# Block inverse: one product over a zero-kept triangle, and products that alternate between row groups and banks

## The chip, the cores and the metric

The kernel runs on one core of a Trainium2 chip. The metric is the time of one execution on the device in microseconds (us). TensorE (PE) multiplies matrices and writes its results to PSUM, VectorE (DVE) and ScalarE (ACT) bring them from there to SBUF, GpSimd (POOL) does small work in SBUF, and SyncE (SP) issues the transfers. Each engine works through its own instructions in order and waits on semaphores of the others.

## The reference

The reference is a stack of blocks over 1024 positions and 1024 channels. The change lies in one of them, a gated delta rule with 8 heads of width 128, cut to what matters here:

```
a_mat = where(strict, (k_beta @ k^T) * decay_mask, 0)     # per head and chunk
t_mat = triangular_solve(a_mat + eye, eye, lower=True)     # its inverse
w = t_mat @ (k_beta * exp(g));  u = t_mat @ v_beta
# then, chunk after chunk:
v_new = u - w @ state
o = q_dec @ state + attn @ v_new
state = state * e_last + k_dec^T @ v_new
```

The kernel uses chunks of 128 positions, so a head has 8 chunks, and 8 lower triangles of 128x128 have to be inverted for each head.

## The kernel before

Most of the kernel's time goes to projections in which a float32 operand is split into two float16 parts (`mm_chT`, lines 111 to 113, and `mm_t`, lines 118 to 120): three products for one. The delta rule lies in the stretch from about 400 to 1000 us. There the program is written head by head: `stage1` (transposes, k·k and q·k products), `base` (blocks of 32x32 inverted by forward substitution on DVE), `levels` (joins the blocks), `chain` (the eight chunks in turn), and `dense(h+2)`, the projections for the head after the next one. In the last heads `zgate`, another projection, takes the place of `dense`. A scheduler of the language sets the order of each engine's instructions from that program; so the projections of `dense` and `zgate` come to stand on TensorE between the small products of `levels` and `chain`.

`levels` holds the inverse of each 128x128 triangle in two layouts: `TdT`, the inverse transposed (an upper triangle), and `Td`, its 32x32 blocks transposed in place. The four diagonal blocks come from `base` through DRAM. Three steps follow. In the first, pairs of blocks of 32 are joined to halves of 64: `ps_x` (line 783) multiplies the block of the strict triangle `U` by one inverse, `X` (784) takes it out of PSUM, `ps_t1` (787) and `ps_t1t` (790) multiply it by the other inverse, for each of the two layouts, and lines 788 and 791 write the results with a minus sign into `Td` and `TdT`. In the second, the two halves are joined: `ps_x2` (796, 797), its copy `X2` (798), `ps_t2t` (801) and its result in `TdT` (802). In the third, `ps_u` and `ps_w` (810) use the finished inverse. The PSUM tiles come from `ps_c`, three banks that are used in turn. In the order and in the trace all the names that begin with ps_t1 or X lose their digit where buffer numbers are left out: `ps_x` is also ps_x2, `ps_t` is ps_t1, `X` is also X2.

Every float32 product shows in the trace as two records of a matmul, so 8 products are 16 records. Operands of 32 rows and 32 columns use one of the sixteen 32x32 parts of the array, those of 64 one of the four 64x64 parts; the part is set by the partitions of the operands (rows) and of the result (columns).

Of the kernel before, what the change touches and what calls it, by code (L numbers as in the profile page):

```python
# [12 lines left out]
AF = mybir.ActivationFunctionType  # L13
ALU = mybir.AluOpType
# [7 lines left out]
NT = 8  # L22
# [6 lines left out]
def kernel(ctx, tc, ins, out):  # L29
    nc = tc.nc  # L30
    pe, dve, act, pool, sp = nc.tensor, nc.vector, nc.scalar, nc.gpsimd, nc.sync
    a = ins
# [16 lines left out]
    def ps_c(n="psc"):  # L49
        return psmm.tile([P, 512], F32, tag="c", name=n, bufs=3)  # L50
# [234 lines left out]
    # ======================= layer 0 =======================  # L285
# [280 lines left out]
    # ======================= layer 1 =======================  # L566
# [14 lines left out]
    with ExitStack() as s0:  # L581
        pl = mkpool("gdn", stack=s0)
        gcol = mkpool("gdnc", stack=s0)
        # decay and beta columns
        wab = load_w(in_w, 4 * D, ncols=16)
        psab = ps_c("ps_ab")
        for i in range(NT):
# [7 lines left out]
        beta = gcol.tile([P, NT, NH], F32, name="beta")  # L595
# [6 lines left out]
                                 op0=ALU.mult, op1=ALU.mult)  # L602
        # exp(-104) is 0 in float32, and so is every decay over such a step
# [22 lines left out]
        TdTs = [pl.tile([P, NT, P], F32, name=f"TdT{i}") for i in range(2)]  # L626
# [5 lines left out]
        # identity columns of the base solves  # L632
# [118 lines left out]
        def base(h):  # L751
            # blocks of 32 by forward substitution, one column group of 8 per partition group
            Lp = st_[h]["Lp"]
            tpd = tp_d[h % 2]
            Tt = gcol.tile([P, 8, 32], F32, tag="Tt", name="Tt")
            tm = gcol.tile([P, 8, 32], F32, tag="tm", name="tm")
            pool.tensor_copy(Tt, tinit)
            for j in range(31):
                n = 31 - j
                tv = tm[:, :, :n]  # L760
                dve.tensor_tensor(out=tv, in0=Lp[:, j, j + 1:].unsqueeze(1).to_broadcast([P, 8, n]),  # L761
                                  in1=Tt[:, :, j:j + 1].to_broadcast([P, 8, n]), op=ALU.mult)
                dve.tensor_tensor(out=Tt[:, :, j + 1:], in0=Tt[:, :, j + 1:], in1=tv, op=ALU.subtract)  # L763
            for q in range(4):
                sp.dma_start(tpd.rearrange("b c m i -> (b c) m i")[:, 8 * q:8 * q + 8, :], Tt[32 * q:32 * q + 32])
            for b in range(4):
                sp.dma_start(TdTs[h % 2][32 * b:32 * b + 32, :, 32 * b:32 * b + 32], tpd[b].rearrange("c m i -> m c i"))

        def levels(h):
            d = st_[h]  # L770
            U, kr, vr, Dc = d["U"], d["kr"], d["vr"], d["Dc"]
            TdT = TdTs[h % 2]
# [3 lines left out]
            # pairs of blocks of 32  # L776
            X = pl.tile([P, NT, 32], F32, tag="X", name="X")
            px, p1, p1t = ps_c("ps_x"), ps_c("ps_t1"), ps_c("ps_t1t")
            v32 = [p[:, :256].rearrange("p (c t) -> p c t", c=NT) for p in (px, p1, p1t)]
            blk = [(slice(r, r + 32), slice(r + 32, r + 64)) for r in (0, 64)]  # L780
            for A, B in blk:
                for c in range(NT):
                    pe.matmul(v32[0][B, c, :], U[A, c, B], Td[A, c, A], start=True, stop=True)
                act.activation(X[B], v32[0][B], AF.Copy)
            for A, B in blk:
                for c in range(NT):
                    pe.matmul(v32[1][B, c, :], TdT[B, c, B], X[B, c, :], start=True, stop=True)
                dve.tensor_scalar(out=Td[B, :, A], in0=v32[1][B], scalar1=-1.0, scalar2=None, op0=ALU.mult)
                for c in range(NT):
                    pe.matmul(v32[2][A, c, :], X[B, c, :], TdT[B, c, B], start=True, stop=True)  # L790
                act.activation(TdT[A, :, B], v32[2][A], AF.Copy, scale=-1.0)
            # halves of 64
            X2 = pl.tile([P, NT, 64], F32, tag="X2", name="X2")
            px = ps_c("ps_x2").rearrange("p (c t) -> p c t", c=NT)
            for c in range(NT):
                pe.matmul(px[hi, c, 0:32], U[lo, c, hi], Td[lo, c, 0:32], start=True, stop=True)
                pe.matmul(px[hi, c, 32:64], U[32:64, c, hi], Td[32:64, c, 32:64], start=True, stop=True)
# [152 lines left out]
    # ======================= hybrid block =======================  # L950
    w_in = a["w_in_2"][0]
    G32, PS, HS, NB = 32, 64, 16, 4
    with ExitStack() as s2:
# [39 lines left out]
        with ExitStack() as s5:  # L993
# [8 lines left out]
            with ExitStack() as s6:  # L1002
# [32 lines left out]
                # growth: exp(lr dt) - 1 through tanh, and its powers  # L1035
# [9 lines left out]
                # angle in turns, range reduced, in two exact parts  # L1045
# [13 lines left out]
                # powers 7..0 and 0..8  # L1059
# [38 lines left out]
                # input matrix: (abar - 1) / lambda * b  # L1098
# [33 lines left out]
                # signed power tables per half  # L1132
# [9 lines left out]
                # skip term on the diagonal of the first tap  # L1142
# [34 lines left out]
            def s5_batch(b):  # L1177
# [6 lines left out]
                # parameters of this batch of groups  # L1184
# [20 lines left out]
                # transposed input maps  # L1205
# [8 lines left out]
                # causal kernel inside a chunk  # L1214
# [14 lines left out]
                # rotation tables and decays  # L1229
# [11 lines left out]
                # inputs by chunk  # L1241
# [278 lines left out]
```

## Time and profile before

| | |
|---|---|
| runs (us) | 1912.77, 1914.98, 1927.49; median 1914.98 |
| profiled execution: span from the first to the last instruction (us), which is the time known of it | 1914.6 |
| TensorE busy, its share of the span | 1808.0 us, 94% |
| DVE, ACT, POOL busy | 76%, 49%, 3% |
| granted TensorE clock, mean over the span | 0.960 |

A busy TensorE is one with a matmul under way; the ends of matmuls are modelled, and the start of the next record tells more of how fast they follow each other than the duration of one. The granted clock is the share of the full 2.4 GHz: 1.00 is that, 0.50 is 1.2 GHz.

### The profile page before, as it was taken

The page shows a single profiled execution, that of the slowest core. Times are in us where ns is not written, and L with a number is a line of the kernel's source. Part 1 is how long each engine was busy: PE and PEld are TensorE (multiplying, and loading weights), DVE is VectorE, ACT ScalarE, POOL GpSimd, SP SyncE. Part 2 cuts the span into 40 slices and gives each one's busy share as a digit, 9 for nine tenths or more (in the row PEclk, how much of TensorE's full clock was granted, in tenths as well). Part 3 has the DMA queues.
Part 4 walks back from the last instruction along what each step waited for, and adds up shares of the span by engine and source line. Part 5 has one row for each costly group of instructions (what it writes and reads, how often), then busy time and mean ns, then how long its engine had stood idle before and what let it go on. Part 6 is the DMA issues. An engine that isn't in the chain of part 4 may idle for free.

```text
span 1914.6 us, 29618 instructions
## 1 busy us (share of the span) xinstructions
PE 1808.0 (94%) x11847; PEld 1133.6 (59%) x11847; DVE 1450.2 (76%) x2472; ACT 935.7 (49%) x1673; POOL 52.8 (3%) x130
## 2 busy tenths in 40 slices
PE   5799789999899999999999999899999999999998
PEld 3344338855466656687878859556444444444487
DVE  6898876655786678877637689999999999594333
ACT  6567563356555666666434443465463121482221
POOL 0000001000000000001000020000000000000000
PEclk8899899999988899999889999999999999999999
DMA  9343255313131131224324322111221112102212
GB/s 336 108 154 85 93 154 188 105 52 84 31 88 39 27 102 30 79 78 138 91 93 155 115 37 71 38 51 53 92 75 54 57 56 77 45 23 66 78 67 89
DMA packets 161635, 165.26 MB, mean 86 GB/s; under 512 B 45662, under 2 KB 139934, under 8 KB 161498
## 3 DMA queue, kind: packets, MB, share of 16 engines
q1 hardware_dynamic: 161498, 163.38, 27.5%
q8 instruction: 93, 1.52, 0.3%
q14 instruction: 44, 0.36, 0.1%
HBM read 139.05 MB, written 23.12 MB: 85 GB/s over the span
## 4 chain that ended last, share of the span: by engine, by line
PE 51%; DVE 29%; ACT 7%; DMA 6%; issue 6%; SPq 1%; POOL 0%; DVEq 0%; ACTq 0%; POOLq 0%
DVE cc L990 5%; PE psmm L112 3%; PE psmm L111 3%; PE psmm L113 3%; DVE wl L105 2%; DMA wst_ada<-in_ada_w_dram 2%; PE ps_out L120 2%; PE ps_out L118 2%; PE ps_out L119 2%; DVE Tt L763 2%; DVE tm L761 2%; PE ps_fin L118 1%; PE ps_fin L120 1%; PE ps_fin L119 1%; PE ps_zc L113 1%
## 5 line engine op out<-in xcount | busy, mean ns | idle before, releaser
L111 PE MATMUL psmm<-hTh,wh 128*128 128x512 f16 x896 | 347.3, 389 | 19.9 <-ACT zs L515 16.7
L112 PE MATMUL psmm<-hTl,wh 128*128 128x512 f16 x896 | 347.6, 388 | 0.1
L113 PE MATMUL psmm<-hTh,wl 128*128 128x512 f16 x896 | 346.4, 387 | 0.0
L990 DVE SCALAR_TENSOR_TENSOR cc<-cu,cols,cc 128x1024 f32<-128x1024 f32 (+1 forms) x270 | 302.2, 1170 | 0.9
L112 PEld LDWEIGHTS <-wh 128*128 128x128 f16 x1568 | 155.0, 99 | 194.7 <-issue 29.5
L113 PEld LDWEIGHTS <-wl 128*128 128x128 f16 x1568 | 155.1, 99 | 179.3 <-issue 13.4
L111 PEld LDWEIGHTS <-wh 128*128 128x128 f16 x1568 | 155.1, 99 | 178.0 <-issue 12.0
L105 DVE SCALAR_TENSOR_TENSOR wl<-wst,wh 128x2048 f16<-128x2048 f32 (+2 forms) x71 | 154.3, 2177 | 57.8 <-ACT wh L104 57.6
L104 ACT ACTIVATE wh<-wst 128x2048 f16<-128x2048 f32 (+2 forms) x71 | 128.6, 1813 | 116.8 <-PE ps_gs L112 27.7
L763 DVE TENSOR_TENSOR Tt<-Tt,tm 128x248 f32<-128x248 f32 (+30 forms) x248 | 77.7, 313 | 4.5
L761 DVE TENSOR_TENSOR tm<-Lp,Tt 128x248 f32<-128x248 f32 (+30 forms) x248 | 76.9, 310 | 4.2
L118 PE MATMUL ps_z<-wh,hTh 128*128 128x256 f16 x256 | 72.1, 282 | 0.0
L119 PE MATMUL ps_z<-wh,hTl 128*128 128x256 f16 x256 | 72.0, 281 | 0.0
L120 PE MATMUL ps_z<-wl,hTh 128*128 128x256 f16 x256 | 71.9, 281 | 0.0
L120 PE MATMUL ps_out<-wl,y 128*128 128x256 f16 x256 | 69.8, 273 | 0.1
L118 PE MATMUL ps_fin<-wh,merged 128*128 128x256 f16 x256 | 69.8, 273 | 0.0
L119 PE MATMUL ps_fin<-wh,merged 128*128 128x256 f16 x256 | 69.8, 273 | 0.0
L120 PE MATMUL ps_fin<-wl,merged 128*128 128x256 f16 x256 | 69.8, 273 | 0.0
L118 PE MATMUL ps_out<-wh,y 128*128 128x256 f16 x256 | 69.7, 273 | 0.0
L119 PE MATMUL ps_out<-wh,y 128*128 128x256 f16 x256 | 69.7, 273 | 0.0
L123 ACT ACTIVATE hTh<-ps_ht 128x512 f16<-128x512 f32 x32 | 17.3, 594 | 83.2 <-PE ps_ht L252 83.2
L701 ACT ACTIVATE jk<-ps_tk 128x128 f32<-128x128 f32 x128 | 35.7, 279 | 39.7 <-PE ps_tk L697 36.7
(535 smaller groups left out, 4171.7 us busy)
## 6 DMA issues: line engine op xcount, KB each, us to landing
wst<-in_w_in_dram SPq DMA_DIRECT2D x24, 1024.0 KB
wst_ada<-in_ada_w_dram SPq DMA_DIRECT2D x16, 1024.0 KB
wst<-in_gdn_in_w_dram SPq DMA_DIRECT2D x16, 1024.0 KB
xt<-in_x_dram SPq DMA_DIRECT2D x16, 512.0 KB
wst<-in_lru_in_w_dram SPq DMA_DIRECT2D x8, 1024.0 KB
sta<-in_ada_w_dram SPq DMA_DIRECT2D x8, 1024.0 KB
x_d<-xt SPq DMA_DIRECT2D x16, 512.0 KB
wst<-in_lru_out_w_dram SPq DMA_DIRECT2D x4, 1024.0 KB
```

Source lines behind the costliest of these rows:

```text
L104: act.activation(hi, st, AF.Copy, scale=WS)
L105: dve.scalar_tensor_tensor(out=lo, in0=st, scalar=WS, in1=hi, op0=ALU.mult, op1=ALU.subtract)
L111: pe.matmul(ps, wh[:, k, c0:c0 + P], ah(k), start=(k == 0), stop=False)
L112: pe.matmul(ps, wh[:, k, c0:c0 + P], al(k), start=False, stop=False)
L113: pe.matmul(ps, wl[:, k, c0:c0 + P], ah(k), start=False, stop=(k == nk - 1))
L118: pe.matmul(ps, ah(k), wh[:, k, :], start=(k == 0), stop=False)
L119: pe.matmul(ps, al(k), wh[:, k, :], start=False, stop=False)
L120: pe.matmul(ps, ah(k), wl[:, k, :], start=False, stop=(k == nk - 1))
L701: act.activation(jk, pst[:, P * c:P * (c + 1)], AF.Square, accum_out=kq[:, n, 4 * b + c:4 * b + c + 1])
L761: dve.tensor_tensor(out=tv, in0=Lp[:, j, j + 1:].unsqueeze(1).to_broadcast([P, 8, n]), in1=Tt[:, :, j:j + 1].to_broadcast([P, 8, n]), op=A ...
L763: dve.tensor_tensor(out=Tt[:, :, j + 1:], in0=Tt[:, :, j + 1:], in1=tv, op=ALU.subtract)
L990: dve.scalar_tensor_tensor(out=acc, in0=cus[j][:, i + t0:i + t0 + n], scalar=col("cw", j, i), in1=acc, op0=ALU.mult, op1=ALU.add)
```

## The change

In `levels` the pairs of blocks of 32 no longer come one after the other. The products of line 783 go to two PSUM tiles instead of one, chunk by chunk in turn between the two pairs; the second pair's copy goes to DVE instead of ACT. The products into `ps_t1` and `ps_t1t` stand in turn too, `ps_t1` of one pair beside `ps_t1t` of the other, so that neighbours use other rows of the array and another bank. The evictions come after all of them.

The join of the halves had two products for each chunk, because the block right above the diagonal of `TdT`'s first half is not zero after the first step of the head two before it (`TdT` is used by every second head). Now POOL sets that block to zero again for every head from the third on, and one product over all 64 rows takes the place of the two. All other differences are comments that are left out.

```diff
             pool.tensor_copy(Tt, tinit)
+            if h >= 2:
+                pool.memset(TdTs[h % 2][0:32, :, 32:64], 0.0)
...
-            px, p1, p1t = ps_c("ps_x"), ps_c("ps_t1"), ps_c("ps_t1t")
-            v32 = [p[:, :256].rearrange("p (c t) -> p c t", c=NT) for p in (px, p1, p1t)]
+            def v32(p):
+                return p[:, :256].rearrange("p (c t) -> p c t", c=NT)
             blk = [(slice(r, r + 32), slice(r + 32, r + 64)) for r in (0, 64)]
-            for A, B in blk:
-                for c in range(NT):
-                    pe.matmul(v32[0][B, c, :], U[A, c, B], Td[A, c, A], start=True, stop=True)
-                act.activation(X[B], v32[0][B], AF.Copy)
-            for A, B in blk:
-                for c in range(NT):
-                    pe.matmul(v32[1][B, c, :], TdT[B, c, B], X[B, c, :], start=True, stop=True)
-                dve.tensor_scalar(out=Td[B, :, A], in0=v32[1][B], scalar1=-1.0, scalar2=None, op0=ALU.mult)
-                for c in range(NT):
-                    pe.matmul(v32[2][A, c, :], X[B, c, :], TdT[B, c, B], start=True, stop=True)
-                act.activation(TdT[A, :, B], v32[2][A], AF.Copy, scale=-1.0)
+            pxs = [v32(ps_c("ps_x")) for _ in blk]
+            for c in range(NT):
+                for (A, B), px in zip(blk, pxs):
+                    pe.matmul(px[B, c, :], U[A, c, B], Td[A, c, A], start=True, stop=True)
+            for n, ((A, B), px) in enumerate(zip(blk, pxs)):
+                if n == 0:
+                    act.activation(X[B], px[B], AF.Copy)
+                else:
+                    dve.tensor_copy(X[B], px[B])
+            p1, p1t = v32(ps_c("ps_t1")), v32(ps_c("ps_t1t"))
+            def t1(n, c):
+                A, B = blk[n]
+                pe.matmul(p1[B, c, :], TdT[B, c, B], X[B, c, :], start=True, stop=True)
+            def t1t(n, c):
+                A, B = blk[n]
+                pe.matmul(p1t[A, c, :], X[B, c, :], TdT[B, c, B], start=True, stop=True)
+            for n in range(2):
+                for c in range(NT):
+                    t1(n, c)
+                    t1t(1 - n, c)
+            for A, B in blk:
+                dve.tensor_scalar(out=Td[B, :, A], in0=p1[B], scalar1=-1.0, scalar2=None, op0=ALU.mult)
+                act.activation(TdT[A, :, B], p1t[A], AF.Copy, scale=-1.0)
...
             for c in range(NT):
-                pe.matmul(px[hi, c, 0:32], U[lo, c, hi], Td[lo, c, 0:32], start=True, stop=True)
-                pe.matmul(px[hi, c, 32:64], U[32:64, c, hi], Td[32:64, c, 32:64], start=True, stop=True)
+                pe.matmul(px[hi, c, :], U[lo, c, hi], Td[lo, c, 0:64], start=True, stop=True)
             dve.tensor_copy(X2[hi], px[hi])
```

The numbers of the changed kernel's lines are higher by 3 in `base`, and by 19 behind the change: 783 is 789 there, 787 and 790 are 799 and 803, 796 and 797 are 816, 801 is 820 and 810 is 829; the evictions 784 are 792 and 794, 788 is 810, 798 is 817, 802 is 821.

Two places show what moves. The first is TensorE in the second head, from the second pair's ps_x to ps_t2t. Before (`psmm` is a projection of `dense`, `ps_qk` a q·k product of `stage1`):

```order
L783 MATMUL ps_x<-Td,U 32x32 x8
L787 MATMUL ps_t_4836<-X,TdT_3594 32x32 x8
L790 MATMUL ps_t1t<-TdT_3594,X 32x32 x8
L113 LDWEIGHTS wl
L113 MATMUL psmm<-hTh,wl 128x512
L745 MATMUL ps_qk<-qT,kT 128x128
L787 MATMUL ps_t_4836<-X,TdT_3594 32x32 x8
L790 MATMUL ps_t1t<-TdT_3594,X 32x32 x8
L796 MATMUL ps_x_4893<-Td,U 64x32
L797 MATMUL ps_x_4893<-Td,U 64x32
```

The same engine and head in the changed kernel, from the last of the 32 alternating products of lines 799 and 803 on:

```order
L799 MATMUL ps_t_4848<-X,TdT_3594 32x32
L803 MATMUL ps_t1t<-TdT_3594,X 32x32
L745 MATMUL ps_qk<-qT,kT 128x128 x3
L816 MATMUL ps_x_4887<-Td,U 64x64 x8
L745 MATMUL ps_qk<-qT,kT 128x128
L111 LDWEIGHTS wh
L111 MATMUL psmm<-hTh,wh 128x512
L112 LDWEIGHTS wh
L112 MATMUL psmm<-hTl,wh 128x512
L745 MATMUL ps_qk<-qT,kT 128x128 x4
```

Three q·k products now stand between the small products and the join, and the rest of them, which stood behind 16 products of lines 796 and 797, is shared out before and behind 8 products of line 816.

The second place is DVE in the same head, from the transposition of `TdT` on. Before (`vT` on line 667 is the convolution of a projection, which no product of this head's levels waits for):

```order
L733 TENSOR_SCALAR rq<-rq 128x8
L667 SCALAR_TENSOR_TENSOR vT<-xp,cols,vT 128x1024
L788 TENSOR_SCALAR Td<-ps_t_4836 32x8x32
L667 SCALAR_TENSOR_TENSOR vT<-xp,cols,vT 128x1024
L788 TENSOR_SCALAR Td<-ps_t_4836 32x8x32
L798 COPY X_4892<-ps_x_4893 64x512
```

And in the changed kernel:

```order
L733 TENSOR_SCALAR rq<-rq 128x8
L794 COPY X<-ps_x 32x256
L667 SCALAR_TENSOR_TENSOR vT<-xp,cols,vT 128x1024
L810 TENSOR_SCALAR Td<-ps_t_4848 32x8x32 x2
L667 SCALAR_TENSOR_TENSOR vT<-xp,cols,vT 128x1024
L817 COPY X_4886<-ps_x_4887 64x512
```

DVE gets one more eviction, and both evictions of `ps_t1` stand together, with a convolution before and one behind them.

## Rows read from the trace of the kernel before

**Rows 1.** The page: busy time and share by engine; share of the chain that ended last.

```profile
PE 1808.0 (94%) x11847; PEld 1133.6 (59%) x11847; DVE 1450.2 (76%) x2472; ACT 935.7 (49%) x1673; POOL 52.8 (3%) x130
...
PE 51%; DVE 29%; ACT 7%; DMA 6%; issue 6%; SPq 1%; POOL 0%; DVEq 0%; ACTq 0%; POOLq 0%
```

**Rows 2.** Stretch with all heads: us, busy of each engine, granted clock, DMA.

```profile
400.00:1000.00 600.00, 581.45 (x4233) 399.64 (x4232) 416.77 (x1075) 349.53 (x906) 25.72 (x47) 0.93 0.25 71
```

**Rows 3.** The eight level blocks, first ps_x to last ps_w: fourth head, and sum.

```profile
709.67:728.69 19.02, 19.02 (x210) 15.04 (x210) 12.31 (x16) 10.31 (x22) 0.20 (x2) 0.91 0.11 29
...
sum 167.32, PE 167.31 PEld 135.85 DVE 88.39 ACT 76.25 POOL 0.61; mean PE 20.91 PEld 16.98 DVE 11.05 ACT 9.53 POOL 0.08
```

**Rows 4.** Waits from 400 to 1000 us: total us, times, longest.

```profile
PE ps_tk L697 <- DVE U L715: 10.8, 5, 5.5
...
DVE X L798 <- PE ps_x L797: 39.3, 8, 6.1
...
DVE TdT L802 <- PE ps_t2t L801: 15.0, 8, 3.0
```

**Rows 5.** Stretches of lines 796 and 797, all eight heads: sum.

```profile
sum 39.36, PE 39.36 PEld 32.12 DVE 1.92 ACT 9.13 POOL 0.00; mean PE 4.37 PEld 3.57 DVE 0.21 ACT 1.01 POOL 0.00
```

**Rows 6.** TensorE in the fourth head by time: start us, duration us, what.

```profile
709.67 0.69 PE L783 MATMUL ps_x<-Td,U 32*32 32x32 f32 x16
710.29 0.39 PE L113 MATMUL psmm<-hTh,wl 128*128 128x512 f16 x1
...
711.28 0.59 PE L783 MATMUL ps_x<-Td,U 32*32 32x32 f32 x13
711.68 0.21 PE L787 MATMUL ps_t<-X,TdT 32*32 32x32 f32 x1
...
711.77 0.19 PE L783 MATMUL ps_x<-Td,U 32*32 32x32 f32 x1
711.80 0.48 PE L787 MATMUL ps_t<-X,TdT 32*32 32x32 f32 x10
...
714.49 0.30 PE L796 MATMUL ps_x<-Td,U 64*64 64x32 f32 x2
714.72 0.30 PE L797 MATMUL ps_x<-Td,U 32*64 32x32 f32 x2
...
721.66 1.14 PE L801 MATMUL ps_t2t<-TdT,X 64*64 64x64 f32 x16
722.74 0.39 PE L111 MATMUL psmm<-hTh,wh 128*128 128x512 f16 x1
```

**Rows 7.** The same engine in the first head, at the granted clock 0.50.

```profile
528.97 0.63 PE L113 MATMUL psmm<-hTh,wl 128*128 128x512 f16 x1
...
529.39 0.63 PE L111 MATMUL psmm<-hTh,wh 128*128 128x512 f16 x1
...
531.24 1.97 PE L801 MATMUL ps_t2t<-TdT,X 64*64 64x64 f32 x16
```

**Rows 8.** The 25 stretches of lines 783, 787 and 790, all eight heads: sum.

```profile
sum 25.63, PE 25.62 PEld 24.54 DVE 13.70 ACT 12.46 POOL 0.20; mean PE 1.02 PEld 0.98 DVE 0.55 ACT 0.50 POOL 0.01
```

**Rows 9.** Behind lines 796, 797 at half clock: first of eight stretches, last, sum.

```profile
528.14:536.97 8.83, 8.83 (x34) 4.03 (x34) 6.46 (x10) 0.00 (x0) 0.00 (x0) 0.50 0.57 147
...
970.27:977.29 7.02, 7.02 (x41) 5.69 (x41) 2.68 (x5) 0.60 (x1) 0.00 (x0) 0.50 0.00 0
sum 49.05, PE 49.05 PEld 35.99 DVE 33.39 ACT 10.75 POOL 0.30; mean PE 6.13 PEld 4.50 DVE 4.17 ACT 1.34 POOL 0.04
```

**Rows 10.** DVE operations: duration ns min/median/max, first and last start us.

```profile
L788 DVE TENSOR_SCALAR Td<-ps_t x16: 417/424/430, 521.9 to 963.8; 32x256 f32<-32x256 f32 x16
...
L798 DVE COPY X<-ps_x x8: 694/695/695, 528.2 to 970.4; 64x512 f32<-64x512 f32 x8
...
L802 DVE TENSOR_SCALAR TdT<-ps_t2t x8: 682/683/683, 533.2 to 974.1; 64x512 f32<-64x512 f32 x8
...
L667 DVE SCALAR_TENSOR_TENSOR vT<-xp,cols,vT x24: 1245/1285/1286, 425.0 to 841.9; 128x1024 f32<-128x1024 f32 x24
```

## The prediction

> **What bounds the kernel now.** I read the page first: TensorE is busy for 94% of the span and holds 51% of the chain that ended last, DVE 76% and 29% [rows 1]. Shares over the whole span hide stages, so next came the stretch that holds all eight heads: of 600 us TensorE is busy 581, DVE 417, ACT 350, POOL 26 [rows 2]. Then the level blocks alone, from the first ps_x of a head to its last ps_w: in the sum of eight, 167.32 us, TensorE is busy for 167.31 and DVE for 88 [rows 3]. The waits say the same from the other side: TensorE's longest wait in the stretch sums to 10.8 us, and not in these blocks, while DVE stands still 39.3 us for the products of lines 796 and 797 and 15.0 us for line 801 [rows 4]. So in these blocks TensorE sets the time, and what it no longer does there comes off the end, as long as the evictions keep up. The projections beside them are work that has to be done anyway; they hide nothing, they queue on the same engine.
>
> Two things make the blocks slow. The products are small, and TensorE's clock falls in or just before lines 796 and 797 of every head: eight stretches behind them, 49.05 us in all, run at 0.50, which is 1.2 GHz [rows 9]. A projection product follows the last one after 0.42 us there [rows 7], where at the full clock it is about half of that.
>
> **The change, part by part.** *The join of the halves.* Lines 796 and 797 now take 39.36 us in the eight heads [rows 5]. At the full clock one of these products costs 0.23 us (714.49 to 714.72), at 64*64 and 32*64 in turn. Line 801 shows what 8 products cost that stay in one shape: 721.66 to 722.74, 1.08 us, 0.135 us each, though each moves 64 columns and not 32 [rows 6]. The new line 816 is 8 products of just that shape. I take 1.08 us a head: 8 x 1.08 = 8.6, a gain of 39.4 - 8.6 = 30.7 us. If they run at half clock, 1.97 us a head [rows 7], the gain is 23.6; if it was not the change of shape that cost, 8 x 8 x 0.23 = 14.7, and the gain is 24.7.
>
> *The products of 32.* They take 25.63 us in all [rows 8], 3.2 us a head for 48 products, 96 records. Inside one line records follow each other by 0.40/13 = 0.031 us, and a stretch costs some 0.12 more when it begins (709.67 to 710.29 is 0.62 for 16). Where the stream passes from the second pair's ps_x to the first pair's ps_t1, other rows and another bank, six records start between 711.68 and 711.80: 0.02 us each, the two lines running beside each other at 0.03 each [rows 6]. If the alternating streams keep 0.016 to 0.02, a head costs 96 x 0.018 + 0.24 = 2.0 us, 16 in all, gain 9.7; if they don't, 96 x 0.031 + 0.24 = 3.2 and the gain is 0. The six are few and had been waiting in the queue, so I take a gain of 8. The Trainium skill (TensorE: Matmul & The Clock Gate, section "Wait — 56ns, not 53.3ns?") says that starts of matmuls never come closer than about 25 ns, however short they are; the starts in the trace, 0.02 apart, are closer than that. By the page alone 96 records cost 2.4 and 0.24 us, and the gain would be some 4 us instead of 8.
>
> *The clock.* With three quarters of lines 796 and 797 gone and projections or q·k products put between, TensorE has less small work in one piece. At worst the clock falls in every head as now, at best in none: then half of the 49.05 us comes back, 24.5. In the fourth head, where twelve q·k products stand between the products of 32, the clock stays up until the last product of line 797, and its blocks take 19.02 us at a mean of 0.91 where the mean of the eight is 20.9 [rows 3]. The changed order mixes like that in heads two to six, so I take two thirds, 16 us.
>
> *New waits.* There are four handovers in a head: X, the two Td, X2, TdT. An eviction takes 0.42, 0.7 or 0.68 us on DVE, and a convolution of 1.28 may stand before it [rows 10]. What covers them on TensorE is less than before: three projections (0.63 us at half of 0.42) behind ps_x, three q·k products behind the alternating ones, where both Td take 0.85 us. The second X copy is new on DVE, 0.42 us a head at most (the price of line 788, an eviction of the same size). The X2 copy has two projections and five q·k products behind line 816 as cover, for its 0.69 us, so nothing there; without them it would be 0.69 a head, 5.6. Beyond the cover I count 0.35 us for X, 0.35 for Td and 0.3 for TdT: 1 us a head, 8 us in all. From below it is 0, since DVE has 167.3 - 88.4 = 79 us free in these blocks [rows 3]; from above 2 us a head, 16, if a convolution stands in the way at each second handover. Behind the waiting evictions DVE has only convolutions and the next head's substitution queued, which it does later instead.
>
> *What costs nothing.* POOL sets the block to zero six times; it is busy 26 of 600 us [rows 2], the block is free once the head two before is through, and only this head's transposition of TdT waits for it; at worst each of the six holds a head up by 25.72/47 = 0.5 us, 3 in all. The two PSUM tiles for ps_x instead of one take a fourth turn of three banks; the first of them has been copied out before ps_t1t needs it, because ps_t1t reads that copy's neighbour. SP's loads of two weights move by a few places; TensorE's longest wait here is on DVE and not on a transfer [rows 4]. The zero triangle adds no columns: 64 moved for one product instead of 32 twice.
>
> The sum: -30.7 - 8 - 16 + 8 = -46.7 us, of the profiled execution's 1914.6: 1867.9. The median of the runs is 1914.98, 0.4 more, so the forecast is **1868 us**, 2.4% faster. By the bounds it lies between 1914.6 - 30.7 - 9.7 - 24.5 = 1850 and 1914.6 - 23.6 + 16 = 1907.
>
> **Rivals.** *The clock falls as before* (1.). The small products still stand closer together than projections do, and new waits put idle time between them. For it: behind the join it is at 0.50 in all eight heads [rows 9]. Against: the fourth head, where the mixing kept it up longest. Then line 816 gains 23.6, the products of 32 gain 8, the clock nothing, the waits cost 8: 1914.6 - 23.6 = 1891.
>
> *The alternation buys nothing* (2.). The records come at 0.031 whatever their rows are, because the instructions can't be given out faster than that. For it: nearly all records do so today; against: the six in rows 6. It takes 8 from the gain: 1876. The page's floor of 25 ns lies between this and the forecast, at 1872.
>
> *The change doesn't do what it says* (3.): the price of line 796 stays with the product of 64, 0.23 us each, the alternation buys nothing and the clock falls: -24.7 + 8, 1898.
>
> *It becomes slower* (4.). TensorE idles at the handovers, the clock falls in each head and stays down for three times as long as in the first head now, because after each return there is another gap: 3 x 8.83 [rows 9] = 26.5 us a head, 212 in all. Now it is between 49, those behind lines 796 and 797, and 49 + 39 = 88, if all of these two lines counts as well; I take 69. Half of the difference, 72 us, is lost, against 23.6 + 8 - 8 = 24 won: 1963. It decides when half-clock time in the heads exceeds 69 + 2 x 24 = 117 us. Against it: the projections behind each block are long and brought the clock back each time, within 9 us in the first head [rows 9].
>
> **How the numbers follow.** The forecast has a chance of 0.50, rival 2 0.14, rival 1 0.20, rival 3 0.11, rival 4 0.05. A measurement of this kernel tells about 1% from no change, 19 us; below 1895.8 is faster by that. The forecast and rival 2 lie below nearly whole (0.63 of 0.64), rival 1 with 0.16 of its 0.20, rival 3 with 0.04 of 0.11: faster 0.83, within 1% 0.12, slower 0.05. For 8 in 10 the range goes from 1850, the sum with every bound on the good side, to 1894, which takes in most of rival 1; outside lie rivals 3 and 4 and the forecast's own tails.
>
> **What would show it.** In the changed profile: 16 records of line 816 in about 1.1 us and no DVE wait of 4 to 6 us for them; 64 records of lines 799 and 803 in 1.1 to 1.4 us, against 2.0 if alternating buys nothing; granted clock 1.00 through most level blocks, so that the stretch of the heads has a mean clock above 0.96; the sum of the eight blocks near 120 us instead of 167; TensorE waits in them, on DVE, of some 8 us. It is wrong if the blocks shrink and TensorE waits instead at ps_tk for the convolutions, which DVE then has still to do: 10.8 us now [rows 4]; more than 30 would mean that DVE sets the pace of a head and most of the gain is given back there.

## The result, and the profile after

The changed kernel takes 1856.84 us in the median of four runs (1854.68 to 1862.81), the kernel before 1917.8 in the median of four. The ratio is 0.9682, with a 95% interval from 0.9656 to 0.9708: 3.2% faster, where 2.4% was forecast. The profiled execution's span falls from 1914.6 to 1853.0, by 61.6 us.

The page answers to [rows 1] so: TensorE is busy for 58 us less, and its share of the chain that ended last falls from 51% to 48%, while DVE's rises from 29% to 33%.

```profile
PE 1750.0 (94%) x11719; PEld 1085.7 (59%) x11719; DVE 1452.2 (78%) x2480; ACT 931.9 (50%) x1665; POOL 54.4 (3%) x136
...
PE 48%; DVE 33%; ACT 7%; issue 6%; DMA 5%; SPq 1%; POOL 0%; DVEq 0%; ACTq 0%; POOLq 0%
```

Where the time went is read best from the stretch of the heads, from its first product (ps_g) to the last end of ps_o. The columns are those of [rows 2]. First the kernel before:

```profile
407.75:994.46 586.71, 569.01 (x4154) 392.18 (x4155) 407.62 (x1049) 341.23 (x894) 25.62 (x46) 0.92 0.25 69
```

and the changed kernel:

```profile
405.47:933.03 527.56, 507.59 (x4028) 342.07 (x4029) 410.53 (x1057) 337.22 (x886) 27.19 (x52) 0.99 0.28 77
```

586.71 - 527.56 = 59.15 of the 61.6 us come from here. The stretch also begins 2.28 us earlier, and what follows it is equal to 0.2 us (1914.6 - 994.46 against 1853.0 - 933.03). The granted clock is up from 0.92 to 0.99, and the time in which TensorE is not busy goes from 17.7 to 20.0 us.

The level blocks of the changed kernel, the fourth head and the sum, answer to [rows 3]:

```profile
682.39:696.01 13.62, 12.89 (x187) 10.77 (x187) 10.77 (x14) 9.07 (x20) 0.40 (x2) 1.00 0.07 22
...
sum 107.93, PE 106.62 PEld 87.61 DVE 87.70 ACT 72.65 POOL 2.51; mean PE 13.33 PEld 10.95 DVE 10.96 ACT 9.08 POOL 0.31
```

The eight blocks take 59 us less than before, and the clock is 1.00 in each of them. DVE does as much as it did and is still not the bound: 87.7 of 107.9.

The windows of line 816, first head and sum of eight, answer to [rows 5]:

```profile
520.62:521.69 1.07, 1.07 (x17) 1.00 (x17) 0.18 (x1) 0.97 (x2) 0.00 (x0) 1.00 0.00 0
...
sum 8.59, PE 8.59 PEld 8.04 DVE 3.53 ACT 5.56 POOL 0.00; mean PE 1.07 PEld 1.01 DVE 0.44 ACT 0.69 POOL 0.00
```

and those of the products of 32, last stretch and sum of 20, to [rows 8]:

```profile
908.99:910.30 1.31, 1.31 (x65) 1.27 (x65) 0.03 (x1) 0.00 (x0) 0.00 (x0) 1.00 0.96 394
...
sum 16.03, PE 16.03 PEld 15.20 DVE 9.14 ACT 7.74 POOL 0.10; mean PE 0.80 PEld 0.76 DVE 0.46 ACT 0.39 POOL 0.01
```

The join costs 39.36 - 8.59 = 30.8 us less, the products of 32 25.63 - 16.03 = 9.6 less. That leaves 59.15 - 30.8 - 9.6 = 18.8 us that all other operations of the stretch lost together, though not one of them was touched. (About 1 of the 9.6 is clock as well: two of the 25 stretches of before, 2.6 us of them, ran at half clock.)

In the first head the alternating products start in pairs (the timeline of TensorE, as [rows 6]):

```profile
518.61 0.21 PE L799 MATMUL ps_t<-X,TdT 32*32 32x32 f32 x1
518.62 0.21 PE L803 MATMUL ps_t1t<-TdT,X 32*32 32x32 f32 x1
518.66 0.19 PE L799 MATMUL ps_t<-X,TdT 32*32 32x32 f32 x1
518.67 0.19 PE L803 MATMUL ps_t1t<-TdT,X 32*32 32x32 f32 x1
518.70 0.19 PE L799 MATMUL ps_t<-X,TdT 32*32 32x32 f32 x1
518.70 0.19 PE L803 MATMUL ps_t1t<-TdT,X 32*32 32x32 f32 x1
```

Each line still has a record every 0.03 us, as before, but there are two lines at once: 64 records take 1.04 us from 518.61 to 519.65.

The waits from 405 to 933 us answer to [rows 4]:

```profile
PE ps_tk L697 <- DVE U L715: 10.5, 5, 5.6
...
DVE X L817 <- PE ps_x L816: 5.6, 6, 1.1
```

DVE's wait for the join falls from 39.3 to 5.6 us, and TensorE's wait at ps_tk has not grown (10.8 before).

### The profile page after: what moved, and what is told of

It reads as the page before. It is cut to its first block, busy times and chain, and to the rows that moved or that the text cites. A ratio compares the mean times of both kernels' runs of the same rounds, so it can differ in the third digit from the quotient of the medians.

```text
span 1853.0 us, 29377 instructions
## 1 busy us (share of the span) xinstructions
PE 1750.0 (94%) x11719; PEld 1085.7 (59%) x11719; DVE 1452.2 (78%) x2480; ACT 931.9 (50%) x1665; POOL 54.4 (3%) x136
## 4 chain that ended last, share of the span: by engine, by line
PE 48%; DVE 33%; ACT 7%; issue 6%; DMA 5%; SPq 1%; POOL 0%; DVEq 0%; ACTq 0%; POOLq 0%
DVE cc L1009 7%; PE psmm L112 3%; PE psmm L111 3%; PE psmm L113 3%; DVE wl L105 3%; DMA wst_ada<-in_ada_w_dram 3%; PE ps_out L120 2%; PE ps_out L118 2%; PE ps_out L119 2%; DVE tm L764 2%; DVE Tt L766 2%; PE ps_fin L120 2%; PE ps_fin L119 2%; PE ps_fin L118 2%; PE ps_zc L111 1%
## 5 line engine op out<-in xcount | busy, mean ns | idle before, releaser
L111 PEld LDWEIGHTS <-wh 128*128 128x128 f16 x1568 | 155.1, 99 | 177.8 <-issue 13.7
L123 ACT ACTIVATE hTh<-ps_ht 128x512 f16<-128x512 f32 x32 | 17.3, 594 | 83.0 <-PE ps_ht L252 83.0
```

The source lines that it names most:

```text
L111: pe.matmul(ps, wh[:, k, c0:c0 + P], ah(k), start=(k == 0), stop=False)
```

## The experiments

Each run changes one thing. What is compared is the ratio to the kernel before, run on the same chip, and, much finer, the stretch of the heads: the changed kernel run again gave 527.61 us for it, against 527.56. Of that stretch the table gives half-clock time (the products that start while the granted clock is at 0.50, each counted up to the next product's start, summed) and the time in products of 32 and in the join (sums of windows as above). Both are of one execution each, the profiled one. In all fourteen traces the clock also falls once during the same idle stretch of TensorE, 5.6 us at ps_tk ahead of the first level block (in the changed kernel from 495.16 to 500.78 us, half clock from 497.57 to 504.40). That half-clock time lies ahead of all the level blocks, and in the changed kernel, e6, e8, e11 and e12 it is all there is.

| kernel | ratio to before, 95% | heads, us | half clock, us | products of 32, us | join, us |
|---|---|---|---|---|---|
| before | | 586.7 | 88.9 | 25.6 | 39.4 |
| changed | 0.9682 (0.9656 to 0.9708) | 527.6 | 3.7 | 16.0 | 8.6 |
| e1 join only | 0.9797 (0.9767 to 0.9827) | 556.4 | 47.6 | 26.8 | 11.4 |
| e2 turns only | 0.9860 (0.9838 to 0.9882) | 566.1 | 51.1 | 15.4 | 31.1 |
| e3 join in two equal products | 0.9709 (0.9690 to 0.9728) | 535.9 | 13.8 | 15.4 | 16.1 |
| e4 before, join grouped | 0.9876 (0.9840 to 0.9913) | 566.2 | 60.5 | 24.9 | 21.2 |
| e5 no turns | 0.9730 (0.9683 to 0.9776) | 548.2 | 36.1 | 23.9 | 11.9 |
| e6 same rows | 0.9631 (0.9605 to 0.9658) | 526.8 | 3.0 | 13.7 | 8.6 |
| e7 join four times | 0.9782 (0.9751 to 0.9812) | 552.2 | 16.2 | 14.8 | 35.8 |
| e8 X on ACT | 0.9670 (0.9644 to 0.9697) | 528.9 | 3.6 | 17.3 | 8.6 |
| e9 one bank | 0.9666 (0.9630 to 0.9702) | 532.9 | 13.7 | 13.3 | 9.4 |
| e10 ps_x three times | 0.9735 (0.9692 to 0.9778) | 543.2 | 13.3 | 27.5 | 9.4 |
| e11 split columns | 0.9638 (0.9595 to 0.9681) | 528.4 | 6.3 | 15.4 | 8.1 |
| e12 changed, again | 0.9668 (0.9628 to 0.9708) | 527.6 | 3.0 | 16.0 | 8.6 |

**The two parts alone.** In e1 the kernel before gets the zeroed block and the one product:

```diff
+            if h >= 2:
+                pool.memset(TdTs[h % 2][0:32, :, 32:64], 0.0)
-                pe.matmul(px[hi, c, 0:32], U[lo, c, hi], Td[lo, c, 0:32], start=True, stop=True)
-                pe.matmul(px[hi, c, 32:64], U[32:64, c, hi], Td[32:64, c, 32:64], start=True, stop=True)
+                pe.matmul(px[hi, c, :], U[lo, c, hi], Td[lo, c, 0:64], start=True, stop=True)
```

> The kernel before with the join alone changed: POOL zeroes the block, one product of 64x64 for each chunk instead of the two; the products of 32 stay pair after pair. Two theories on what held TensorE's clock down in every head of the kernel before. Shape theory: the turns between parts of 64 and of 32 rows in lines 796 and 797 hold the stream, and the clock falls because of them; then without them the clock stays up and the join gives its 30.8 us and nearly all of the 18.7 us that the other operations of the heads lost: 48 to 50 us below the kernel before, half-clock time in the heads under 10 us. Stretch theory: it is all the small work that stands in one piece, the products of 32 as well; then the clock still falls in about half of the heads, half-clock time 25 to 45 us, and the gain is 30.8 + 9 = about 40 us or less (down to 24 if it falls in all).

In e2 the same two edits are undone in the changed kernel, and the turns stay:

```diff
-            if h >= 2:
-                pool.memset(TdTs[h % 2][0:32, :, 32:64], 0.0)
-                pe.matmul(px[hi, c, :], U[lo, c, hi], Td[lo, c, 0:64], start=True, stop=True)
+                pe.matmul(px[hi, c, 0:32], U[lo, c, hi], Td[lo, c, 0:32], start=True, stop=True)
+                pe.matmul(px[hi, c, 32:64], U[32:64, c, hi], Td[32:64, c, 32:64], start=True, stop=True)
```

> The changed kernel with the old join: two products for each chunk, of 64 and of 32 rows in turn, no zeroing on POOL; the products of 32 in turns over rows and banks stay. Shape theory: the clock falls in every head as in the kernel before (half-clock time in the heads 70 to 90 us); gained are the 9.6 us of the products of 32, less up to 8 us of new waits: 2 to 10 us below the kernel before, 1905 to 1913. Stretch theory: with q.k products and projections mixed in and 1.2 us a head less of small work the clock falls in half of the heads at most, half-clock time 25 to 45 us: 25 us or more below the kernel before, under 1890.

The stretch of the heads, in e1 and then in e2:

```profile
411.44:967.87 556.43, 533.82 (x4019) 365.25 (x4020) 406.92 (x1049) 339.25 (x894) 27.26 (x52) 0.95 0.27 73
```

```profile
416.94:983.01 566.07, 547.63 (x4150) 368.25 (x4151) 412.17 (x1057) 337.62 (x886) 24.30 (x46) 0.95 0.26 72
```

Alone, the join gains 30.3 us of the stretch and the turns 20.6, together 50.9; both at once gain 59.15, so 8.2 us come only with both. The clock shows why: each part alone takes half-clock time from 89 to about 50 us, both take it to 4. The shape theory (the turns between two shapes hold the clock down) wanted under 10 us in e1 and 70 to 90 in e2, and falls on both. The stretch theory (it is all the small work that stands in one piece) comes nearer: e1 is 37 us below the kernel before (1891.94 against 1928.83; about 40 or less expected) and e2 25 (1904.26; 25 or more and under 1890 expected), with half-clock time a little above its 45 us in both.

**What in the join was dear.** e3 makes the join two products again, of equal shape, in the changed kernel:

```diff
-                pe.matmul(px[hi, c, :], U[lo, c, hi], Td[lo, c, 0:64], start=True, stop=True)
+                pe.matmul(px[hi, c, 0:32], U[lo, c, hi], Td[lo, c, 0:32], start=True, stop=True)
+                pe.matmul(px[hi, c, 32:64], U[lo, c, hi], Td[lo, c, 32:64], start=True, stop=True)
```

> The changed kernel, but the join is again two products of 32 columns for each chunk, both over all 64 rows of the zero-kept triangle: 16 products a head as in the kernel before, 32 records, all of one shape. Shape theory: records of one shape follow each other as closely as those of 64 columns at worst (0.067 us): 32 x 0.067 = 2.1 us a head at most instead of 1.07, so 4 to 9 us above the changed kernel, and the clock stays up in all heads. Count theory (the old lines were slow because there were 16 products and not 8): 0.23 us a product as before, 3.6 us a head, 20 us above the changed kernel, and 19 us more if the clock falls: 1877 to 1896.

e4 leaves the kernel before as it is, but for the order of the join:

```diff
                 pe.matmul(px[hi, c, 0:32], U[lo, c, hi], Td[lo, c, 0:32], start=True, stop=True)
+            for c in range(NT):
                 pe.matmul(px[hi, c, 32:64], U[32:64, c, hi], Td[32:64, c, 32:64], start=True, stop=True)
```

> The kernel before with one edit: all eight products of line 796 (64 rows) come first, then all eight of line 797 (32 rows): the same products, no zero block, one change of shape a head instead of fifteen. Shape theory: eight at 0.07 to 0.135 us, eight at 0.03 to 0.135, and one change: 1 to 2.3 us a head instead of 4.9, and the clock stays up mostly: 39.4 - 13 = 26 us and 15 to 19 us of clock, 40 to 45 us below the kernel before. Count theory: no change, within 5 us of the kernel before, half-clock time in the heads 80 to 90 us.

TensorE by time in e3, where lines 816 and 817 have one shape, two records each:

```profile
528.41 0.28 PE L817 MATMUL ps_x<-Td,U 64*64 64x32 f32 x2
528.52 0.28 PE L816 MATMUL ps_x<-Td,U 64*64 64x32 f32 x2
528.64 0.28 PE L817 MATMUL ps_x<-Td,U 64*64 64x32 f32 x2
528.76 0.28 PE L816 MATMUL ps_x<-Td,U 64*64 64x32 f32 x2
```

and in e4, first head, at the full clock, where 796 is followed by what was 797:

```profile
527.76 1.11 PE L796 MATMUL ps_x<-Td,U 64*64 64x32 f32 x16
528.80 1.11 PE L798 MATMUL ps_x<-Td,U 32*64 32x32 f32 x16
529.85 0.39 PE L111 MATMUL psmm<-hTh,wh 128*128 128x512 f16 x1
```

A product of 32 columns starts 0.12 us after the last one in e3 and costs 1.04/8 = 0.13 in e4, and one of 64 columns 1.07/8 = 0.134 in the changed kernel: the columns moved hardly count. Nor do the rows by themselves: line 798 of e4 has 32 rows in a part of 32*64 and takes 1.05 us, as much as 64 rows do, where 16 records in a part of 32*32 take 0.61 (line 799 alone). The join with its fifteen changes of shape stands wholly at the full clock in the first head of e2:

```profile
532.16:535.80 3.64, 3.64 (x33) 2.99 (x33) 1.41 (x2) 0.97 (x2) 0.00 (x0) 1.00 0.11 26
```

So the join's price had two parts. Sixteen products cost 2.0 to 2.1 us a head in one shape (e3) or grouped in two (e4); the same sixteen with fifteen changes of shape cost 3.64: (3.64 - 2.09)/15 = 0.10 us a change. The other part is the number: 8 instead of 16, 1.0 us a head. The Trainium skill (TensorEngine Tiling (Array Packing), section Key Properties) says that changing the tiling mode drains TensorE; these 0.10 us a change agree. The shape theory is right on e3's time of the join (16.05 us, 2.0 a head, within its bound of 2.1) and on its distance from the change (8.4 us of the heads, within 4 to 9), though the clock, wanted up in all heads, falls in the last one. It is right on e4's join too (within 2.3 at the full clock; with half-clock time 21.2 us instead of 13). It is wrong on e4's clock, which it wanted mostly up and which is down for 60 us; so e4 lies 23 us below the kernel before and not 40 to 45. The count theory (the old join was dear because it had 16 products) is wrong on both.

**What in the turns counts.** In e5 nothing stands in turns; the eight products of one pair come first, in lines 789, 799 and 803 alike:

```diff
-            for c in range(NT):
-                for (A, B), px in zip(blk, pxs):
+            for (A, B), px in zip(blk, pxs):
+                for c in range(NT):
                     pe.matmul(px[B, c, :], U[A, c, B], Td[A, c, A], start=True, stop=True)
...
                 for c in range(NT):
                     t1(n, c)
+                for c in range(NT):
                     t1t(1 - n, c)
```

> The changed kernel with the products of 32 not in turns: for each of the three steps all eight of one pair, then all eight of the other (for line 799 and line 803 still the one pair beside the other). PSUM tiles, evictions, the order of engines around them and the new join stay. Rate: records 0.031 us instead of 0.02, 3.2 us a head instead of 2.0: 9.6 us above the changed kernel by itself; if the turns don't matter, 0. The clock: the runs so far ordered the kernels by the small work of a head (before 7.9 us at full clock: 89 us of half-clock time; grouped join 6.4: 60; turns alone 6.6: 51; join alone 5.3: 48; two equal products 5.1: 14; changed kernel 4.1: 4), but the last two also have other work between the pieces. Amount theory: 5.3 us a head, as with the join alone, so 40 to 50 us at half clock and 20 us more: about 30 us above the changed kernel, ratio to before 0.983. Mixing theory: the order of the work between is that of the changed kernel, so the clock stays up, half-clock time under 20 us, 10 to 15 us above the changed kernel, ratio 0.973 to 0.976.

In e6 the neighbours in the turns are of one pair:

```diff
-                    t1t(1 - n, c)
+                    t1t(n, c)
```

> The changed kernel with one edit: in the turns of lines 799 and 803 both neighbours are of the same pair, so they use the same 32 rows of the array, other columns and another bank (line 789 stays as it is). If it takes other rows: 64 records a head at 0.031 us instead of 0.016 to 0.02, 1.0 us a head, 7 to 8 us above the changed kernel and perhaps 5 to 10 for the clock: ratio 0.972 to 0.977. If another bank or other columns are enough: no difference, 0.968.

e9 is e6 with one PSUM tile for both results:

```diff
-            p1, p1t = v32(ps_c("ps_t1")), v32(ps_c("ps_t1t"))
+            p1 = v32(ps_c("ps_t1"))
+            p1t = p1
```

> The kernel of e6 (lines 799 and 803 in turns within a pair, so with the same rows of the array), and now with one PSUM tile for both results, so in the same bank as well: neighbours differ in the columns of the array alone, and in the partitions they write. Column theory: each part of the array takes its products one after the other, about 0.031 us a record for 32 rows, and parts with other columns run beside each other; then nothing changes, 64 records in 1.0 to 1.2 us a head, within 4 us of the changed kernel. Bank theory: the turns pay because of the banks; then 0.031 us a record again, 2.0 us a head, 7 us more, and some half-clock time with it: 10 to 25 us above the changed kernel.

The windows of all products of 32 in e5, their sum, and the heads of e5:

```profile
sum 23.91, PE 23.91 PEld 23.08 DVE 11.21 ACT 10.07 POOL 0.10; mean PE 1.26 PEld 1.21 DVE 0.59 ACT 0.53 POOL 0.01
```

```profile
407.25:955.44 548.19, 529.41 (x4034) 362.25 (x4035) 411.51 (x1057) 337.13 (x886) 25.62 (x52) 0.97 0.27 74
```

Without the turns the products of 32 cost 7.9 us more, and the clock falls again in four heads. Half-clock time is 36.1 us, between the amount theory's 40 to 50 and the mixing theory's under 20; the ratio is the latter's (0.973), the heads are 20.6 us longer than the change's, between 10 to 15 and 30. Neither is right as it was put. In the level blocks of the second and third heads the order of the other work on TensorE is exactly that of the changed kernel, and the clock falls in both, so mixing alone doesn't hold it; in the other heads the order differs by a few products. The fall isn't certain either: of e5's four runs one, of 1866.65 us, had a mean clock of 0.981, as the changed kernel's runs have (0.980 to 0.984), and the other three, of 1876 to 1884 us, had 0.973 or 0.974.

The windows of the alternating products alone, first head, in e6 and in e9:

```profile
527.62:528.66 1.04, 1.04 (x65) 1.00 (x65) 1.01 (x2) 1.04 (x3) 0.10 (x1) 1.00 0.00 0
```

```profile
524.34:525.38 1.04, 1.04 (x66) 1.00 (x65) 1.01 (x2) 1.04 (x3) 0.10 (x1) 1.00 0.00 0
```

Neither other rows nor another bank is needed: with the same rows, and then with the same bank too, 64 records take the 1.04 us of the changed kernel. Other columns are enough. Whether other rows with the same columns would be enough as well, no run tests. The trace of the kernel before could have told the first part: in its first head line 787 passes to line 790 of the same pair, with the same rows, and there the starts are as close:

```profile
521.63 0.21 PE L790 MATMUL ps_t1t<-TdT,X 32*32 32x32 f32 x1
521.66 0.19 PE L787 MATMUL ps_t<-X,TdT 32*32 32x32 f32 x1
521.68 0.19 PE L790 MATMUL ps_t1t<-TdT,X 32*32 32x32 f32 x1
521.69 0.19 PE L787 MATMUL ps_t<-X,TdT 32*32 32x32 f32 x1
```

The Trainium skill (TensorE: Matmul & The Clock Gate, Part 3, section "The mechanism") says that a weight load overlaps products under way only when its row group differs. In e6 the row group is the same, and each product brings its own weights; by the rate these loads overlap all the same. e9's stretch is 5.3 us longer than the change's, a little over the 4 us expected, with waits that the shared tile brings (ps_t2t on ACT's copy, 2.1 us) and the clock down in two heads; its ratio is the same within its interval. e6 is shorter by 0.8 us in the heads and by 2.3 in the products of 32: there all 64 records always stand in turns, while in four heads of the changed kernel eight products of line 799 come alone (0.61 us a stretch), and in the last one some do.

e11 cuts the products of 64 columns into two column parts:

```diff
-                pe.matmul(px[hi, c, :], U[lo, c, hi], Td[lo, c, 0:64], start=True, stop=True)
+                for s in (0, 32):
+                    pe.matmul(px[64 + s:96 + s, c, :], U[lo, c, 64 + s:96 + s], Td[lo, c, 0:64], start=True, stop=True)
...
-                pe.matmul(px[lo, c, :], X2[hi, c, :], TdT[hi, c, hi], start=True, stop=True)
+                for s in (0, 32):
+                    pe.matmul(px[s:s + 32, c, :], X2[hi, c, s:s + 32], TdT[hi, c, hi], start=True, stop=True)
```

> The changed kernel with each product of lines 816 and 820 cut in two halves of 32 result partitions, in turns: 64x32 parts, 32 products and 64 records a head more in place of 32. Were the price one of a record in its part of the array whatever its columns (0.067 us), the two column parts would run beside each other, and the same work would take as long as before: 1.07 us a line and head, no change within 4 us. If a record with half the columns costs half, 0.5 us a line and head are saved: 8 us below the changed kernel. If starts can't come closer than 0.067 us for these sizes, each line takes 2.1 us: 17 us above.

The line 817 of e11 in the first head:

```profile
531.54 1.08 PE L817 MATMUL ps_x<-Td,U 64*32 64x64 f32 x32
```

32 records take what 16 took, the sum of the join is 8.14 us against 8.59. The first expectation is right: a record of 64 rows takes its part of the array for some 0.065 us, with 32 or 64 columns, and two parts with other columns run beside each other.

**What brings the clock down.** e7, with the first of these edits, and e10, with the second, add small work to the changed kernel and nothing else; both write the same values again into the same place:

```diff
+                for r in range(4):
                     pe.matmul(px[hi, c, :], U[lo, c, hi], Td[lo, c, 0:64], start=True, stop=True)
```

> The changed kernel with each product of line 816 issued four times in a row (the same values into the same place): 32 products of 64x64 a head, 64 records at 0.067 us, 4.3 us instead of 1.07; nothing else differs. By itself 8 x 3.2 = 26 us above the changed kernel. Amount theory: small work of 7.3 us a head, near the 7.9 of the kernel before, so the clock falls in most heads, 60 to 90 us at half clock, 25 to 35 us more: 50 to 60 us above the changed kernel, ratio to before 0.996. Mixing theory, or that it takes products of 32 rows or a change of shape: the clock stays up, half-clock time under 20 us, 26 to 32 us above, ratio 0.982 to 0.985.

```diff
-            for c in range(NT):
+            for c, r in [(c, r) for c in range(NT) for r in range(3)]:
                 for (A, B), px in zip(blk, pxs):
                     pe.matmul(px[B, c, :], U[A, c, B], Td[A, c, A], start=True, stop=True)
```

> The changed kernel with each product of line 789 issued three times (the same values into the same place), in turns between the pairs: 96 records a head in place of 32, at 0.02 us each, 1.9 us instead of 0.63: 10 us above the changed kernel by itself. All the products of 32 then take 3.3 us a head, as much as in e5 where they stand one line after the other. If it is the time spent in products of 32 that brings the clock down, half-clock time in the heads is about 36 us as in e5, and the kernel is 10 + 15 = 25 us above the changed one. If it is the slow row of products in a single part of the array, the clock stays up, half-clock time under 15 us, and the kernel is 10 to 12 us above.

The heads of e7, and then of e10:

```profile
416.73:968.91 552.18, 532.28 (x4405) 366.43 (x4406) 411.22 (x1057) 337.01 (x886) 26.32 (x52) 0.98 0.27 74
```

```profile
415.85:959.09 543.24, 521.63 (x4542) 353.73 (x4543) 410.87 (x1057) 338.74 (x886) 26.68 (x52) 0.99 0.27 75
```

e7 has nearly as much small work in a head as the kernel before (7.3 us against 7.9 by its expectation), and the clock stays up in the level blocks of seven heads. In the eighth it falls in the middle of line 817, at 939.21 us, within an idle time of TensorE that e7's own timeline puts down to nothing but issue:

```profile
935.76 1.61 PE L817 MATMUL ps_x<-Td,U 64*64 64x64 f32 x24
940.12 4.42 PE L817 MATMUL ps_x<-Td,U 64*64 64x64 f32 x40 [2.76 <-issue]
```

In e10 too seven of the eight heads keep the clock, and its last head also holds an idle stretch, of 2.4 us, among the products of 32 (27.49 us of windows with 25.11 busy); the clock falls 0.3 us after it. No other idle stretch over 0.25 us in the heads of any of the fourteen traces is put down to issue, and in each of the two a 16 KB packet of the DMA queue that the page calls instruction (q8) starts just after TensorE has stopped, at 937.88 us in e7 and at 929.03 in e10. So TensorE may have waited there for its own instructions; no run tests that. With these two falls set aside, neither the amount of small work nor the time in products of 32 brings the clock down; the amount theory falls. Each of the kernels with 36 to 89 us at half clock (before, e1, e2, e4, e5) has at least one of two things: products of 32 rows that stand one after the other in a single part of the array, at 0.03 us a record, or changes of shape at each product. The kernels that have neither, but for eight products of line 799 in some heads (changed, e3, e6 to e12), have 3 to 16 us. That is how the profiled executions sort, and the mean clocks of all runs over their spans sort alike (0.954 to 0.974 for before, e1, e2 and e4; 0.976 to 0.984 for the second group), but for e5, which reaches from 0.973 to 0.981. It isn't a mechanism: in e5 four heads keep the clock with the same products as the other four, and in e3 it falls in the last head, in the join, with no idle time there. Why the clock falls among busy small products stays open.

**The second copy of X.** In e8 both copies of ps_x are ACT's.

```diff
-                if n == 0:
-                    act.activation(X[B], px[B], AF.Copy)
-                else:
-                    dve.tensor_copy(X[B], px[B])
+                act.activation(X[B], px[B], AF.Copy)
```

> The changed kernel with both copies of ps_x on ACT (two activations after each other) instead of one on ACT and one on DVE. If DVE's queue (a convolution of 1.28 us may stand ahead) is what the alternating products wait for, ACT is no worse and the time falls by 1 to 4 us; if the two copies side by side are worth their 0.42 us, it rises by 8 x 0.4 = 3 us. By either less than 5 us from the changed kernel, ratio 0.966 to 0.970.

528.9 us against 527.6 for the heads, ratio 0.967: no difference that the times can tell, as either expectation had it. The copy on DVE is neither a gain nor a burden here.

**The change again.**

> The changed kernel itself, on the chip of the other runs of this group, so that they can be set against it: ratio to the kernel before 0.966 to 0.971, half-clock time in the heads under 10 us. A theory in which the clock stayed up by luck in its profiled execution gives 20 us or more of half-clock time here.

As expected, 0.9668, and 3.0 us at half clock. e6 and e11 have lower ratios (0.9631, 0.9638), but against 0.9668 and 0.9682 the intervals overlap or touch, and their heads differ from the change's by less than 1 us. No run shows a version that is faster than the change.

## Why the prediction was right, and where it was off

The measured median lies in the range, 11 us below the forecast. By its own steps:

- *The join*, forecast -30.7 us: 39.36 to 8.59, -30.8. The price that was taken, that of line 801, is the one that line 816 has, 1.07 us a head. What the prediction left together under "stay in one shape" e2, e3 and e4 took apart: at the full clock about 1.6 us a head for fifteen changes of shape and 1.0 for half the products; the rest, 39.36 - 8 x 3.64 = 10.2 us, is half-clock time, which stood in lines 796 and 797 as well.
- *The products of 32*, -8 with -9.7 as the good end: -9.6. The records came at 0.016 us in turns, the good end; the eight products that stand alone in four heads took some of it away (11.03 us for lines 799 and 803, 1.38 a head, at the upper end of the 1.1 to 1.4 named). The reason given, other rows and another bank, was not the one that counts: e6 and e9 have neither and lose nothing, so other columns are enough. The Trainium skill's floor of 25 ns between starts (TensorE: Matmul & The Clock Gate, section "Wait — 56ns, not 53.3ns?"), by which 4 us were to come, doesn't hold for such neighbours: 64 records in 1.04 us are 0.016 apart.
- *The clock*, -16: this is the term that was mis-sized. "So I take two thirds" was too low; the clock stays up in all eight blocks, not in two of three. All other operations of the heads lost 18.8 us net, where -16 + 8 = -8 was forecast, and this makes up most of the difference between 46.7 and 59.2. Outside the join and the products of 32 half-clock time falls from 88.9 - 29.4 - 2.6 = 56.8 us (the 49.05 of [rows 9] and 7.8 elsewhere) to 3.7, worth 26.6 at most. The prediction gave two reasons, less small work in one piece and other work mixed in, as in the fourth head before. Neither holds by itself: e7 has nearly the small work of before and keeps the clock in seven heads, e5 has the mixing and loses it in four. As long as the mechanism is open, it is in part luck that the clock came out on the good side.
- *New waits*, +8: mis-sized too. What shows is 2.3 us more of idle time of TensorE in the stretch (17.7 to 20.0), 1.3 of it in the blocks (0.01 to 1.31). If that is all, the clock and whatever else changed gave 18.8 + 2.3 = 21.1 us. That 26.6 - 18.8 = 7.8 comes near 8 proves nothing, since 26.6 is an upper bound.
- *What costs nothing*: POOL's six zeroings take 0.30 us each, and nothing is seen to wait for one of them, in the changed kernel or in e1; and DVE stays off the path (87.7 of 107.9 us in the blocks; ps_tk waits 10.5 us where 30 would have meant that DVE sets the pace).
- The rivals: the clock didn't fall as before (1.), the alternation buys 9.6 us (2.), line 816 costs 0.134 us a product and not 0.23 (3.), and nothing of 4. shows. Each would have been seen in the rows named ahead: 1.07 us a head for line 816, 1.38 for the alternating products, 0.99 for the clock, DVE's waits of at most 1.1 us. Two signs came out otherwise: the blocks take 107.9 us and not about 120, and TensorE waits in them for 1.3 us and not for 8.

The other 2.4 us of the 61.6 lie ahead of and behind the heads, in stages that the change doesn't touch; in the other runs' profiles the heads begin anywhere from 407 to 417 us.

## What to carry to other kernels

Price a small product by its record in its part of the array, not by its columns: look in the timeline for how far starts are apart in a row of one shape, and for what a change of shape adds, before counting multiplications; zeros that let two shapes become one can be free. Neighbours that write to other columns ran beside each other here, without a second bank or other rows. And where the granted clock is low behind a group of small products, its price stands on all the other lines: each part alone gave somewhat under half of it back here and both together nearly all, so such edits are worth trying together.

## What was not expected of the hardware

- Two 32x32 parts of the same rows, with other columns, take records at 0.016 us together, into the same bank too (e9); one alone takes them at 0.031.
- A change between parts of 64*64 and of 32*64 costs 0.10 us each time (e2 against e4).
- A record of 64 rows takes 0.06 to 0.067 us, whether 32 or 64 columns are moved (e3, line 816) and whether it fills 32 or 64 columns of the array (e11). One of 32 rows takes as much in a part of 32*64 (e4, 1.05 us for 16) and about half in one of 32*32.
- 64 records of 64*64 in one row, 3.9 us of them, left the clock at 1.00 in the level blocks of seven heads (e7); in e5 it fell in four heads whose products of 32 stood one line after the other.
- With more instructions TensorE stood still for 2.76 us in the midst of line 817 in one head, with nothing to wait for but issue (e7), and for 2.38 us in e10; in both a 16 KB packet of the instruction queue starts just after it has stopped.
